# Scaling and transposing finished row pairs at other steps of the first down projection

## The chip, the core and the metric

The kernel runs on one core of a Trainium2 chip. The engines that matter here, with the names of the profile: PE (TensorE, matrix products; PEld is its loading of the stationary operand), DVE (VectorE), ACT (ScalarE), POOL (GpSimd) and SP (SyncE, which here only issues transfers). ACT issues transfers too; a transfer that stands in an engine's queue appears as ACTq or SPq. Every engine works through its own queue in order. If the instruction at the head of a queue waits for another engine or for a transfer, everything behind it on that engine waits too.

The metric is the time of one execution in device microseconds (us); less is better. Of several executions the median is given. The output must agree with the reference, in fp32.

## The reference

A trunk of two layers works on 256 context tokens and 1024 latent tokens, each a row of 1024 numbers. Each layer has a mixing part (attention beside a state-space scan, with a common input projection) and a feed-forward part. The change sits between the feed-forward part of the first layer and the input projection of the second. Cut to this stretch:

```python
def rmsnorm(x, w):
    xf = x.astype(jnp.float32)
    y = xf * lax.rsqrt(jnp.mean(xf * xf, axis=-1, keepdims=True) + EPS)
    return (y * w.astype(jnp.float32)).astype(x.dtype)

# end of layer 0; the same for the context rows with their own g2, w and gains
x = x + g2 * rmsnorm((silu(f @ w_gate) * (f @ w_up)) @ w_down, norm_ffn_post)
# start of layer 1
h = rmsnorm(x, norm_mix_pre) * (1 + sc1) + sh1
... h @ w_in ...
```

So a finished row of the down projection (`@ w_down`, 2816 inputs, 1024 outputs) is normalised, gated and added to its old value. The new row is normalised again, scaled and shifted, and multiplied by the next weights.

## The kernel before, in words

**Products.** Every fp32 number is kept as a high and a low part, and a product is three matrix products in a row (`mm3`): high by high at line L224, high by low at L225, low by high at L226. Weights come as fp32 through SP (L125, 512 KB for a step of the down projection). ACT makes the high part (L114), POOL the low part (L115). There are five buffers for split weights (`w_t`) and two for raw ones (`raw_t`).

**The down projection** (`down_all`). The ten blocks of 128 rows, called tiles here, are worked through in three groups: tiles 0 to 3, then 4 to 6, then 7 to 9. Tiles 0 and 1 are the context rows. These are groups 0, 1 and 2 below. In a group the inner loop runs over 22 steps `ff`, each with 128 of the 2816 inputs. A tile has two PSUM banks of 128x512, so a step of a group with three tiles has 3 x 2 x 3 = 18 matrix products. The `hid` operand of a step is loaded by SP at L1197 into `hid_ring`, eight steps ahead. PSUM has two pools, one of five banks (`ps_w`) and one of three (`ps_s`). A group of three tiles takes four of the one and two of the other, so one bank of each is left over.

**The end of a group.** At step 21 each tile goes through `finish_psum` and `postnorm`. ACT squares its two banks (L239), POOL forms the reciprocal root of the mean (`rstd_t`, L241, L231, L232), DVE multiplies the banks by it and by the gate row into an `xt` buffer (L828, the two instructions that free the banks). SP loads the old row (L825). The two are added at L834, by POOL for even tiles and by DVE for odd ones, and ACT's queue stores the sum at L835. There are six `xt` buffers.

**The pairs.** When the second tile of a pair (0 and 1, 2 and 3, 4 and 5, 6 and 7, 8 and 9) is finished, `done` prepares the pair for layer 1. `pre_scale` squares the new rows (ACT, L239, two for each tile), forms `rstd_t` on POOL and scales the rows in place there (L371). Because it writes in place, L371 also waits until the store L835 of the same buffer has landed. `flip_steps` then transposes the pair in four steps. A step has four transposes on PE (L398) into one `ps_w` bank, two scale-and-shift instructions on ACT (L401), the high part on POOL (L405) and the low part on DVE (L406):

```python
    def pre_scale(self, xs):
        for a in xs:
            r = self.row_rstd(...)                  # ACT L239 x2, POOL L241, L231, L232
            for b in ...:
                self.nc.gpsimd.tensor_scalar(b, b, r, 1.0, op0=ALU.mult, op1=ALU.mult)   # L371
```

In the program `down_all` calls `fill` after each step of groups 1 and 2, and `fill` takes one of the waiting flip steps. Whatever is left after group 2 is handed on as `late`. The input projection of layer 1 (`xbc(1)`) runs it inside the first column blocks, before the matrix products that need the last span of rows (`hb`, tiles 6 to 9). Its products are copied out of PSUM by ACT (L479).

**What sets the order.** The program's text is only a start. A scheduler simulates the engines and writes each engine's queue, so a change of the text moves instructions on all five queues. The rows of these queues are shown below.

Of the kernel before, what the change touches and what calls it, by code (L numbers as in the profile page):

```python
# [54 lines left out]
class Trunk:  # L55
# [1146 lines left out]
    def down_all(self, l, hx, load, fill=lambda: None, done=lambda t, x: None):  # L1202
        loads = self.loads
        ahead = 9 if l else 8
        for n in range(3, ahead):
            load(n)
        for n, (g, ff) in enumerate(loads):
            ts = self.GROUPS[l][g]
            if ff == 0:
                banks = [[a(), b()] for a, b in ((self.psw, self.psw), (self.psw, self.psw), (self.pss, self.pss), (self.psw, self.pss))[:len(ts)]]  # L1210
            h, u = hx.pop(n), self.U[l, "d", g, ff]
            for i, t in enumerate(ts):
                for c in range(2):
                    s = slice(c * 512, (c + 1) * 512)
                    self.mm3(banks[i][c], (h[:, 0, i * P:(i + 1) * P], h[:, 1, i * P:(i + 1) * P]), (u[:, 0, 0, s], u[:, 1, 0, s]),
                             ff == 0, ff == NFF - 1)
                if ff == NFF - 1:
                    done(t, self.finish_psum(l, t, banks[i]))
            self.free(l, "d", g, ff)
            load(n + ahead)  # L1220
            if g:
                fill()

    def finish_psum(self, l, t, halves):
# [7 lines left out]
def emit(nc, tc, I, out, dump=None):  # L1232
    with ExitStack() as es:
        k = Trunk(nc, tc, es, I, out)
        k.hT, k.fgrow = {}, (None, None)
        k.plan()
        SC, SA, SB = k.SPANS
        tiles = list(range(NT))
        step = lambda g: lambda *a: next(g, None)
        k.silu_c()  # L1240
        flips = [k.pre_pair(SC, 0, -1, 0, 0), k.pre_pair(SA, 0, -1, 0, 0)]
        k.mod_first()
        k.pump()
        flips[0]()
        flips[1]()
        k.pre_pair(SA, 1, -1, 0, 0)()
        late = [lambda i=i: k.pre_pair(SB, i, -1, 0, 0)() for i in range(2)]
        def drain(*gs):
            for g in gs:
                for _ in g:  # L1250
                    pass

        for l in range(DEPTH):
            ms = k.mod_stream(0, (2, 3, 4), k.psw) if l == 0 else iter(())
            k.load_qkw(l)
            k.xbc(l, step(ms), late)
            with tc.tile_pool(name=f"kv{l}", bufs=1, reuse_waits="tile") as kv:
                k.dt_raw = k.cst.tile([P, NT, 8], F32, tag="dt_raw", name="dt_raw")
                qt = tiles if l == 0 else tiles[NCT:]
                tab = k.rope_tab(k.x(), "k_norm", l)  # L1260
                k.w_tok(l, "kv", 264, tiles, lambda t, p: k.kv_proc(l, t, p, tab), step(ms))
                k.ssd_prep(l, kv)
                tabq = k.rope_tab(k.grp.tile([P, D], F32, tag="grow", name="rope_q"), "q_norm", l)
                st = k.ssd_states(l, kv)
                k.w_tok(l, "q", 512, qt, lambda t, p: k.q_proc(l, t, p, tabq), lambda: (next(ms, None), next(st, None)))
                drain(ms, st)
                cols = k.mod_cols(l, 1)
                fl = {}

                def early(stage):  # L1270
                    keep = k.hf_d[l]
                    if stage == 0:
                        cols()
                        fl[0] = k.pre_pair(SC if l == 0 else SA, 0, 2 * l, l, 1, keep if l else None)
                        if l:
                            fl[2] = [k.row_halves(t, 2) for t in (6, 7)]
                    elif stage == 1:
                        fl[0]()
                        fl[1] = k.pre_pair(SA, l, 2 * l, l, 1, keep)
                        if l:  # L1280
                            k.pre_scale(fl[2])
                    else:
                        fl[1]()
                        if l == 0:
                            fl[2] = k.pre_pair(SA, 1, 0, 0, 1, keep)

                gate, ss = k.ssd(l, kv)
                zf = itertools.chain([step(ss)] * (len(qt) - 1), [lambda: None])
                nz = iter(range(len(qt)))
                att = []  # L1290

                def zfill():
                    i = next(nz)
                    if i == 2:
                        k.att_keys(l)
                    if i == len(qt) - 4:
                        k.att_open(l)
                    if i == len(qt) - 2:
                        att.append(k.attention(l, early))
                        next(att[0])  # L1300
                    next(zf)()

                k.qs = {}
                k.w_tok(l, "z", 512, qt, gate, zfill)
                att = att[0]
                next(att)
                for _ in ss:
                    next(att)
            with tc.tile_pool(name=f"att{l}", bufs=1, reuse_waits="tile") as atp:
                try:  # L1310
                    att.send(atp)
                except StopIteration:
                    pass
            if dump and dump(k, l):
                return
            with tc.tile_pool(name=f"acc{l}", bufs=1, reuse_waits="tile") as accp:
                if l == 0:
                    B = {}

                    def fill_c():  # L1320
                        fl[2]()
                        yield
                        xs = [k.row_halves(t, 0) for t in (6, 7)]
                        B.update(k.blocks(accp))
                        yield
                        for i in range(2):
                            k.pre_scale(xs)
                            yield
                            for _ in k.quads(0, xs, i, B):
                                yield  # L1330
                            if i == 0:
                                xs = [k.row_halves(t, 0) for t in (8, 9)]
                                yield

                    fc = fill_c()
                    k.ctx_gateup(0, fc)
                    drain(fc)
                    k.back22(B)

                    def fill_s():  # L1340
                        yield from k.mod_stream(0, (5,), k.psw, True)
                        yield from k.mod_stream(1, (0, 1), k.psw, True)
                        cols = k.mod_cols(1, 0)
                        yield from k.mod_stream(1, (2,), k.psw, True)
                        cols()
                        yield from k.mod_stream(1, (3, 4, 5), k.psw, True)

                    fs = fill_s()
                    hx, load = k.ffn(0, B, step(fs), accp)
                    drain(fs)  # L1350
                    k.frow = [k.gate_row(0, 5, "norm_ffn_post", 0), k.gate_row(0, 5, "norm_ffn_post", 1, k.x())]
                    ys, todo = {}, []
                    pairs = {1: (SC, 0), 3: (SA, 0), 5: (SA, 1), 7: (SB, 0), 9: (SB, 1)}

                    def done(t, y):
                        ys[t] = y
                        if t in pairs:
                            xs = [ys[t - 1], y]
                            k.pre_scale(xs)
                            todo.append(k.flip_steps(xs, *pairs[t], 1, 0))  # L1360

                    def flip():
                        while todo and next(todo[0], todo) is todo:
                            todo.pop(0)

                    k.down_all(0, hx, load, flip, done)
                    late = [lambda: drain(todo.pop(0))] * len(todo)
                else:
                    B = k.blocks(accp)
                    B["B22"] = k.block22()  # L1370
                    k.down_all(1, *k.ffn(1, B, lambda: None, accp, fl[2], [k.last_x[t] for t in (8, 9)]))
# [23 lines left out]
```

## Time and profile before

| | us |
|---|---|
| median of 3 runs | 3227.97 |
| lowest and highest of them | 3227.72, 3238.06 |
| the profiled execution's own time | 3234.53 |
| its span in the trace | 3232.7 |
| PE busy in it | 3041.5 (94%) |
| the down projection's group 1 (from 1626.4 to 1725.3) | 98.9 |
| the down projection's group 2 (from 1725.3 to 1832.5) | 107.2 |

The trace is one execution, and its times are counted from the start of its span. Its own time is 6.56 us above the median. What is outside the span is 3234.53 - 3232.7 = 1.83 us. A row of a timeline gives the start, the duration, the engine, the line, the operation, its output and input, how many like it follow one another, and in brackets how long the engine had stood idle before and what ended that. A row of windows gives the stretch, its length, the busy time with the number of instructions, the granted PE clock (1.00 is full), the share of the transfer engines that was busy, and GB/s. `L371` is line 371 of the kernel before.

### The profile page before, as it was taken

Reading aid. Unit: us, or ns where it says so; the run is one execution under the profiler, and the core shown is the slowest. Engines: PE = TensorE matmul, PEld = TensorE weight load, DVE = VectorE, ACT = ScalarE, POOL = GpSimd, SP = SyncE. Lnnn points to the kernel's source line nnn. Section 1 sums busy time; section 2 is a strip of 40 time slices with the busy share of each in tenths; the row PEclk is TensorE's granted clock in tenths of the full one; section 3 lists DMA queues with packets and bytes.
Section 4 is the critical chain, followed back from the end, with each engine's and each line's share of the span. In section 5 each row is a group of like instructions: output and inputs, shape, how many; then the busy total and the mean of one; then the engine's idle time right before and its main releaser. Section 6 shows DMA issues by size and latency. Waiting matters only on the chain.

```text
span 3232.7 us, 44982 instructions
## 1 busy us (share of the span) xinstructions
PE 3041.5 (94%) x16147; PEld 2517.7 (78%) x16147; DVE 1665.7 (52%) x3093; ACT 1410.9 (44%) x2595; POOL 1663.6 (51%) x1529
## 2 busy tenths in 40 slices
PE   6899899999888999999998998899999899999997
PEld 4677688888787777778876778788888688888885
DVE  2557556777553655553021156759665766554003
ACT  4433337667653333332143344337666633333232
POOL 4327465555654444444476643755444555554653
PEclk8899899999999999999999999999999899999999
DMA  6267553222565554446566515653222443336766
GB/s 229 71 216 229 188 171 105 84 66 72 170 207 179 169 189 156 171 170 235 181 227 230 169 51 166 216 172 113 66 66 79 137 131 117 111 110 209 237 241 213
DMA packets 372703, 510.66 MB, mean 158 GB/s; under 512 B 25400, under 2 KB 258520, under 8 KB 372224
## 3 DMA queue, kind: packets, MB, share of 16 engines
q1 hardware_dynamic: 292912, 385.09, 37.9%
q10 hardware_dynamic: 79568, 122.69, 10.3%
q8 instruction: 128, 2.10, 0.3%
q14 instruction: 95, 0.78, 0.1%
HBM read 384.71 MB, written 122.99 MB: 157 GB/s over the span
## 4 chain that ended last, share of the span: by engine, by line
PE 73%; DMA 9%; DVE 6%; POOL 5%; ACT 3%; issue 3%; SPq 0%; ACTq 0%; DVEq 0%; POOLq 0%
PE ps_w L224 11%; PE ps_w L225 11%; PE ps_w L226 11%; PE ps_s L224 7%; PE ps_s L225 7%; PE ps_s L226 7%; PE ps_w L912 5%; PE ps_w L905 4%; PE ps_s L883 4%; POOL w_t L115 3%; DMA raw_t<-in_w_down 2%; DMA raw_t<-in_w_up 2%; ACT w_t L114 1%; PE ps_w L275 1%; PE ps_w L755 1%
## 5 line engine op out<-in xcount | busy, mean ns | idle before, releaser
L115 POOL TENSOR_TENSOR w_t<-raw_t,w_t 128x512 fp32r<-128x512 f32 (+2 forms) x430 | 795.7, 1861 | 834.3 <-ACT w_t L114 806.1
L114 ACT CAST w_t<-raw_t 128x512 fp32r<-128x512 f32 (+2 forms) x490 | 389.3, 810 | 774.4 <-PE ps_s L226 240.5
L884 DVE TENSOR_SCALAR_CACHE_REDUCE att_a<-ps_s 128x512 f32<-128x512 f32 (+1 forms) x400 | 227.0, 586 | 138.4 <-PE ps_s L883 128.1
L892 POOL TENSOR_SCALAR att_a<-att_a,att_st 128x1280 f32<-128x1280 f32 (+1 forms) x144 | 181.7, 1264 | 152.3 <-DVE att_st L891 84.2
L225 PE MATMUL ps_w<-w_t,hid_ring 128*128 128x512 f32 x523 | 207.5, 397 | 8.6 <-POOL w_t L115 8.6
L226 PE MATMUL ps_w<-w_t,hid_ring 128*128 128x512 f32 x523 | 206.3, 395 | 0.0
L224 PE MATMUL ps_w<-w_t,hid_ring 128*128 128x512 f32 x523 | 195.9, 395 | 3.7 <-ACT w_t L114 3.1
L905 PE MATMUL ps_w<-cst_all,att_a 128*128 128x128 f32 x1312 | 198.4, 277 | 0.0
L890 ACT ACTIVATE att_a<-att_a,att_st 128x1280 f32<-128x1280 f32 (+1 forms) x144 | 183.2, 1273 | 32.9 <-DVE att_st L889 30.6
L485 DVE SCALAR_TENSOR_TENSOR xt<-row,convw,xt 128x512 f32<-128x512 f32 (+1 forms) x128 | 125.1, 1031 | 84.5 <-ACT xt L483 66.0
L905 PEld LDWEIGHTS ps_w<-cst_all,att_a 128*128 128x128 f32 x1312 | 153.9, 142 | 10.7 <-DVE xt L828 5.4
L828 DVE SCALAR_TENSOR_TENSOR xt<-ps_w,rstd_t,gate_row 128x512 f32<-128x512 f32 x57 | 40.0, 746 | 230.8 <-POOL rstd_t L232 168.8
L115 DVE TENSOR_TENSOR w_t<-raw_t,w_t 128x1024 fp32r<-128x1024 f32 (+1 forms) x60 | 69.9, 1173 | 168.9 <-ACT w_t L114 168.9
L115 DVE TENSOR_TENSOR xt<-s2t,xt 128x512 fp32r<-128x512 f32 (+2 forms) x144 | 121.7, 846 | 48.2 <-ACT xt L114 46.6
L114 ACT CAST xt<-s2t 128x512 fp32r<-128x512 f32 (+2 forms) x144 | 78.0, 542 | 147.3 <-DVE s2t L1141 61.9
L224 PE MATMUL ps_w<-ha,w_t 128*128 128x512 f32 x352 | 138.5, 394 | 2.3 <-ACT xt L1016 2.3
L225 PE MATMUL ps_w<-ha,w_t 128*128 128x512 f32 x352 | 138.8, 394 | 2.0 <-DVE ha L406 2.0
L226 PE MATMUL ps_w<-ha,w_t 128*128 128x512 f32 x352 | 138.2, 393 | 0.0
L225 PEld LDWEIGHTS ps_w<-w_t,hid_ring 128*128 128x128 f32 x523 | 98.9, 189 | 34.0 <-POOL w_t L115 12.0
L224 PE MATMUL ps_w<-hc,w_t 128*128 128x256 f32 x352 | 106.1, 302 | 19.6 <-ACT w_t L114 17.6
L224 PEld LDWEIGHTS ps_w<-w_t,hid_ring 128*128 128x128 f32 x523 | 98.7, 189 | 26.8 <-ACT w_t L114 4.0
L226 PEld LDWEIGHTS ps_w<-w_t,hid_ring 128*128 128x128 f32 x523 | 98.9, 189 | 21.4
(364 smaller groups left out, 8771.3 us busy)
## 6 DMA issues: line engine op xcount, KB each, us to landing
raw_t<-in_w_down SPq DMA_DIRECT2D x132, 512.0 KB
hid<-xt ACTq DMA_DIRECT2D x88, 512.0 KB
raw_t<-in_w_gate SPq DMA_DIRECT2D x70, 512.0 KB
raw_t<-in_w_up SPq DMA_DIRECT2D x66, 512.0 KB
hid_ring<-hid SPq DMA_DIRECT2D x85, 384.0 KB
xt<-in_w_mod SPq DMA_DIRECT2D x56, 512.0 KB
xt<-xs SPq DMA_DIRECT2D x36, 512.0 KB
raw_t<-in_w_in SPq DMA_DIRECT2D x32, 512.0 KB
```

The source lines that it names most:

```text
L114: self.nc.scalar.copy(hi, src)
L115: (eng or self.nc.vector).tensor_tensor(lo, src, hi.bitcast(F32), op=ALU.subtract)
L224: mm(out, st[0], mv[0], start=first, stop=False)
L225: mm(out, st[0], mv[1], start=False, stop=False)
L226: mm(out, st[1], mv[0], start=False, stop=last)
L485: nc.vector.scalar_tensor_tensor(acc, row[:, o0 + k:o0 + k + n], cw[:, ct, k:k + 1], acc, op0=ALU.mult, op1=ALU.add)
L883: nc.tensor.matmul(s[:, :m], qs[t][c][:, hd], kst[:, g, j:j + m], start=c == 0, stop=c == 1)
L884: nc.vector.tensor_scalar(pb[:, j:j + m], s[:, :m], -0.125, None, op0=ALU.mult, op1=ALU.min, accum_out=st[:, n:n + 1])
L890: nc.scalar.activation(pb, pb, AF.Exp, bias=nmx, scale=-1.0, accum_out=st[:, 4:5])
L892: nc.gpsimd.tensor_scalar(pb, pb, st[:, 5:6], 1.0, op0=ALU.mult, op1=ALU.mult)
L905: nc.tensor.transpose(tp[:, (2 * k + h) * P:(2 * k + h + 1) * P], pr[h][:, (k2 + k) * P:(k2 + k + 1) * P], self.ident)
L912: nc.tensor.matmul(av, vst[:, kt, g], pt[:, c, k * 256:(k + 1) * 256], start=kt == 0 and c == 0, stop=kt == nk - 1 and c == 1)
```

## The change

A small generator, `ready`, stands for a pair in the list of waiting work. Its first call runs `pre_scale`, its second does nothing, and calls three to six are the four flip steps. `fill` is no longer called after step 0 of a group.

```diff
@@ down_all @@
             self.free(l, "d", g, ff)
             load(n + ahead)
-            if g:
+            if g and ff:
                 fill()
@@ emit @@
+                    def ready(xs, span, i):
+                        k.pre_scale(xs)
+                        yield
+                        yield
+                        yield from k.flip_steps(xs, span, i, 1, 0)
+
                     def done(t, y):
                         ys[t] = y
                         if t in pairs:
-                            xs = [ys[t - 1], y]
-                            k.pre_scale(xs)
-                            todo.append(k.flip_steps(xs, *pairs[t], 1, 0))
+                            todo.append(ready([ys[t - 1], y], *pairs[t]))
```

In the program's text this gives, for each pair:

| pair | scaled before | first flip before | scaled now | flips now |
|---|---|---|---|---|
| 0, 1 | end of group 0 | group 1, step 0 | group 1, step 1 | group 1, steps 3 to 6 |
| 2, 3 | end of group 0 | group 1, step 4 | group 1, step 7 | group 1, steps 9 to 12 |
| 4, 5 | end of group 1, before tile 6 is finished | group 1, step 21 | end of group 1, after tile 6 is finished | group 2, steps 2 to 5 |
| 6, 7 | group 2, step 21, before tile 8 | group 2, step 21 | group 2, step 21, after tile 9 | in `late` |
| 8, 9 | group 2, step 21 | in `late` | in `late` | in `late` |

The number of instructions on PE is the same. In the rows below a name ends in its buffer's number.

**PE, from group 1 into group 2, before.** `ps_s_15183` is a bank of tile 9, `ps_w_15179` the first of tile 7, `xt_15101` the row block of tile 4, `w_t_15011` the weight of step 0 and `w_t_15165` that of step 4.

```order
L226 MATMUL ps_s_15183<-w_t_15059,hid_ring_13732 128x512
L224 MATMUL ps_s_15183<-w_t_15083,hid_ring_13733 128x512
L225 MATMUL ps_s_15183<-w_t_15083,hid_ring_13733 128x512
L226 MATMUL ps_s_15183<-w_t_15083,hid_ring_13733 128x512
L224 MATMUL ps_s_15183<-w_t_15165,hid_ring_13732 128x512
L225 MATMUL ps_s_15183<-w_t_15165,hid_ring_13732 128x512
L226 MATMUL ps_s_15183<-w_t_15165,hid_ring_13732 128x512
L398 MATMUL ps_w_15169<-cst_all_84,xt_15101 128x128
L224 MATMUL ps_w_15179<-w_t_15011,hid_ring_13732 128x512
```

**The same place now.** The queue of group 2 begins with steps 0 to 3 on two banks. The first transpose of the pair stands behind 81 matrix products of the group:

```order
L224 MATMUL ps_w_15171<-w_t_15149,hid_ring_13732 128x512
L225 MATMUL ps_w_15171<-w_t_15149,hid_ring_13732 128x512
L398 MATMUL ps_w_15247<-cst_all_84,xt_15101 128x128
L226 MATMUL ps_w_15171<-w_t_15149,hid_ring_13732 128x512
L224 MATMUL ps_w_15172<-w_t_15149,hid_ring_13732 128x512
L225 MATMUL ps_w_15172<-w_t_15149,hid_ring_13732 128x512
L226 MATMUL ps_w_15172<-w_t_15149,hid_ring_13732 128x512
L398 MATMUL ps_w_15247<-cst_all_84,xt_15121 128x128
```

Before, the transpose of tile 4 stands in front of the group's first matrix product on a `ps_w` bank, after 15 products on one `ps_s` bank. Now it stands well inside step 4 (`w_t_15149`).

**ACT at the same boundary, before.** `xt_15101` and `xt_15121` are the rows of tiles 4 and 5, `ps_s_14499` and `ps_s_14500` the banks of tile 6.

```order
L114 CAST w_t_15165<-raw_t_15163 128x1024
L835 DMA xs1_96<-xt_15101 128x1024
L835 DMA xs1_96<-xt_15121 128x1024
L239 ACTIVATE junk_90,ss_t_15127<-xt_15101 128x512 x2
L239 ACTIVATE junk_90,ss_t_15135<-xt_15121 128x512 x2
L239 ACTIVATE junk_90,ss_t_15150<-ps_s_14499 128x512
L239 ACTIVATE junk_90,ss_t_15150<-ps_s_14500 128x512
```

**And now** (the banks of tile 6 are `ps_s_14467` and `ps_s_14468`):

```order
L239 ACTIVATE junk_90,ss_t_15134<-ps_s_14467 128x512
L114 CAST w_t_15149<-raw_t_15147 128x1024
L239 ACTIVATE junk_90,ss_t_15134<-ps_s_14468 128x512
L835 DMA xs1_96<-xt_15121 128x1024
L835 DMA xs1_96<-xt_15101 128x1024
L239 ACTIVATE junk_90,ss_t_15153<-xt_15101 128x512 x2
L239 ACTIVATE junk_90,ss_t_15161<-xt_15121 128x512 x2
```

The squares of tile 6 have moved ahead of those of the pair, and the store of tile 5 ahead of that of tile 4.

**PE in the first column blocks of layer 1, before.** `ha` and `hc` are spans of the transposed rows, `w_t_15640` and `w_t_15663` the weights of the first and second block, `xt_15157` and `xt_15726` the rows of tiles 6 and 7.

```order
L226 MATMUL ps_s_15881<-ha_14662,w_t_15640 128x512
L398 MATMUL ps_w_15810<-cst_all_84,xt_15157 128x128
L398 MATMUL ps_w_15810<-cst_all_84,xt_15726 128x128
L398 MATMUL ps_w_15810<-cst_all_84,xt_15157 128x128
L398 MATMUL ps_w_15810<-cst_all_84,xt_15726 128x128
L224 MATMUL ps_s_15907<-hc_14525,w_t_15663 128x256
```

**And now:**

```order
L224 MATMUL ps_s_15854<-ha_14782,w_t_15640 128x512
L225 MATMUL ps_s_15854<-ha_14782,w_t_15640 128x512
L226 MATMUL ps_s_15854<-ha_14782,w_t_15640 128x512
L224 MATMUL ps_s_15880<-hc_14581,w_t_15663 128x256
L225 MATMUL ps_s_15880<-hc_14581,w_t_15663 128x256
```

The four transposes have left this place. All 32 transposes of the pairs 6, 7 and 8, 9 now stand in a row behind the eight column blocks of `hc` and `ha`, where 28 stood before.

## The prediction

> **What bounds the kernel now.** I read the page's shares of busy time first, then its chain of waits.
>
> ```profile
> PE 3041.5 (94%) x16147; PEld 2517.7 (78%) x16147; DVE 1665.7 (52%) x3093; ACT 1410.9 (44%) x2595; POOL 1663.6 (51%) x1529
> PE 73%; DMA 9%; DVE 6%; POOL 5%; ACT 3%; issue 3%; SPq 0%; ACTq 0%; DVEq 0%; POOLq 0%
> ```
>
> PE is busy 94% of the span and makes most of the chain. The change adds and removes no PE instruction, so it can win only PE's idle time and slow clock, or add to them. Next, what PE waited for in groups 1 and 2 and at their start (1500 to 1850 us of the span):
>
> ```profile
> PE ps_w L398 <- POOL xt L371: 12.0, 2, 8.3
> PE ps_s L225 <- POOL w_t L115: 1.9, 1, 1.9
> PE ps_w L224 <- ACT w_t L114: 1.6, 1, 1.6
> PE ps_w L225 <- POOL w_t L115: 0.8, 1, 0.8
> PE ps_w L224 <- DVE xt L828: 0.6, 1, 0.6
> ```
>
> Columns: total us, times, longest. Twelve us are two waits of a transpose for the in-place scaling L371, exactly the two instructions that the change pulls apart. PE's timeline places them:
>
> ```profile
> 1725.27 0.40 PE L224 MATMUL ps_s<-w_t,hid_ring 128*128 128x512 f32 x1
> 1730.37 0.56 PE L225 MATMUL ps_s<-w_t,hid_ring 128*128 128x512 f32 x1 [1.90 <-POOL w_t L115]
> 1739.64 0.47 PE L398 MATMUL ps_w<-cst_all,xt 128*128 128x128 f32 x1 [8.28 <-POOL xt L371]
> 1845.43 0.55 PE L398 MATMUL ps_w<-cst_all,xt 128*128 128x128 f32 x3 [3.68 <-POOL xt L371]
> ```
>
> From 1725.27 to 1730.37 PE had only 15 products on the one free `ps_s` bank. Then the transpose of tile 4 stood at the head of its queue, while the banks behind it were free already: the four L828 that free those of tiles 4 and 5 ended at 1730.25. The windows give the price (us, PE busy, clock, DMA share, GB/s):
>
> ```profile
> 1728.50:1739.60 11.10, 0.99 (x2) 0.60 0.85 323
> 1739.60:1744.50 4.90, 4.86 (x13) 0.52 0.01 2
> 1725.30:1832.50 107.20, 97.02 (x414) 0.94 0.60 196
> 1801.60:1831.00 29.40, 29.40 (x127) 1.00 0.47 135
> 1626.40:1725.30 98.90, 96.44 (x429) 1.00 0.71 239
> ```
>
> After the stall the clock stays at 0.52 for 4.90 us. Undisturbed, seven steps of 18 products take 29.40 us: 4.20 a step, 0.2333 a product.
>
> **Term 1, the boundary of groups 1 and 2.** Twenty-two steps make 92.4 us. The pair's 16 transposes fall in this group in both kernels. Later 28 of them take 3.33 us in a row:
>
> ```profile
> 1872.75 3.33 PE L398 MATMUL ps_w<-cst_all,xt 128*128 128x128 f32 x28
> ```
>
> That is 0.12 each, 1.9 for 16. Of 107.2 us, 107.2 - 92.4 - 1.9 = **12.9 us** are lost: 1.90 + 8.28 of idle time, and most of the rest at the slow clock, where 13 instructions took 4.86 us and should take 12 x 0.2333 + 0.12 = 2.9.
>
> Does the new order meet another wait there? PE's new queue has 26 products on two free banks, then those on the banks of tiles 4 and 5, needed from 1725.27 + 26 x 0.2333 = 1731.3 on. They were free by 1730.25, with DVE doing the same four L828 in the same order:
>
> ```profile
> 1727.52 2.73 DVE L828 SCALAR_TENSOR_TENSOR xt<-ps_w,rstd_t,gate_row 128x512 f32<-128x512 f32 x4 [35.57 <-POOL rstd_t L232]
> 1732.96 1.23 DVE L834 TENSOR_TENSOR xt<-xt 128x1024 f32<-128x1024 f32 x1 [2.72 <-DMA xt<-xs]
> 1742.84 1.41 DVE L828 SCALAR_TENSOR_TENSOR xt<-ps_s,rstd_t,gate_row 128x512 f32<-128x512 f32 x2 [8.65 <-POOL rstd_t L232]
> ```
>
> The second bank of tile 6 is needed after 55 products, at 1738.1. Its L828 stands on DVE behind L834 of tile 5, which waited for the transferred old row and ended at 1734.19; plus 1.41 gives 1735.6. That is 2.5 us in time.
>
> The first transpose stands after 81 products: 1744.2; the one of tile 5 at 1745.1. When are those rows scaled?
>
> ```profile
> 1730.28 2.34 POOL L834 TENSOR_TENSOR xt<-xt 128x1024 f32<-128x1024 f32 x1
> 1738.47 1.12 POOL L371 TENSOR_SCALAR xt<-xt,rstd_t 128x1024 f32<-128x1024 f32 x1 [1.23 <-DMA xs<-xt]
> 1732.65 1.89 ACTq L835 DMA_DIRECT2D xs<-xt  x2
> 1734.59 0.63 ACT L239 ACTIVATE junk<-xt 128x512 f32<-128x512 f32 x1 [7.62 <-DVE xt L834]
> 1737.60 0.60 ACT L239 ACTIVATE junk<-ps_s 128x512 f32<-128x512 f32 x1
> ```
>
> The first L371 waited for the store of its buffer, 1738.47 - 1732.65 = 5.8 us after the issue. ACT's queue now issues tile 5's store first, after 1734.2, and tile 4's about 1735.2; 5.8 later is 1741.0. The four squares take 1737.60 - 1734.59 = 3.0 and end at 1738.2, their `rstd_t` is there about 1739.5, and POOL's L834 of tile 6, put ahead of both L371, is done by 1735.6 + 2.34 = 1738.0. So the store sets the time: L371 at 1741.0 and 1742.1, done at 1742.1 and 1743.2. **The margins are 2.1 and 1.9 us.** So I take nothing as a new stall here, with the two ends 0 and 2 us for what can eat the margin:
>
> ```profile
> 1835.32 2.78 DVE L834 TENSOR_TENSOR xt<-xt 128x1024 f32<-128x1024 f32 x1
> 1837.00 2.09 POOL L371 TENSOR_SCALAR xt<-xt,rstd_t 128x1024 f32<-128x1024 f32 x1
> ```
>
> The same two operations that took 1.23 and 1.12 took 2.78 and 2.09 when they ran over one another. Two L371 stretched so are 1.9 us. [...]
>
> The weights: step 5's buffer comes free when step 0's last product ends, after about 58 of them, at 1738.9. Its low part then takes these two conversions:
>
> ```profile
> 1725.93 1.04 ACT L114 CAST w_t<-raw_t 128x1024 fp32r<-128x1024 f32 x1
> 1727.96 2.35 POOL L115 TENSOR_TENSOR w_t<-raw_t,w_t 128x1024 fp32r<-128x1024 f32 x1
> ```
>
> The raw buffers are filled ahead, so only the two conversions follow the release: 1738.9 + 1.04 + 2.35 = 1742.3. PE needs it at 1746.8. Steps 6 and 7 have 5 to 6 us in hand by the same count.
>
> **Term 2, group 1.** In the window of 98.9 us PE was busy for 96.44, which 396 products (92.4) and 32 transposes (3.8) explain: 2.5 are lost, 1.62 + 0.79 = 2.4 of them in pauses for late weights. SP is why:
>
> ```profile
> 1633.33 9.32 SPq L825 DMA_DIRECT2D xt<-xs  x2
> 1659.38 1.20 PE L224 MATMUL ps_w<-w_t,hid_ring 128*128 128x512 f32 x4 [1.62 <-ACT w_t L114]
> ```
>
> Two loads of old rows waited 9.32 us for buffers, with weight loads queued behind. In the new order the weights of steps 4 to 7 come, by the same working as above, 6 to 8 us before PE needs them, since two banks are worked four steps ahead. I take **-2.4**; the ends are 0 and -2.5.
>
> **Term 3, the end of group 2 and layer 1's first blocks.** The 3.68 us wait goes, because the four transposes leave that place, and with it the slow clock behind it:
>
> ```profile
> 1832.40:1835.40 3.00, 3.00 (x25) 2.83 (x23) 1.49 (x3) 1.05 (x1) 2.78 (x18) 1.00 0.77 203
> 1845.43:1850.18 4.75, 4.75 (x27) 4.75 (x28) 3.56 (x5) 1.02 (x2) 4.39 (x8) 0.64 0.00 0
> ```
>
> A block of 24 products of 256 columns takes 2.9 us at full clock (25 in 3.00), and three transposes 0.4; here the 27 took 4.75 at 0.64: 1.4 lost. Gain 5.1. Against it:
>
> ```profile
> 1835.91 0.50 PE L224 MATMUL ps_s<-ha,w_t 128*128 128x512 f32 x1 [0.46 <-ACT row L479]
> 1872.75:1879.60 6.85, 4.30 (x33) 3.45 (x31) 3.90 (x5) 6.65 (x15) 4.18 (x6) 1.00 0.00 0
> 1873.43 6.49 ACT L401 ACTIVATE s2t<-ps_w,cols 128x256 f32<-128x256 f32 x14
> ```
>
> The first copy L479 comes later on ACT, estimated behind one square more (0.60 as above, and its read-out): 0.7 beyond the 0.46. A `ps_s` bank of tile 9, freed behind the same squares, is late by an estimated 0.5. Eight flip steps instead of seven stand before the `hb` products, and ACT, 14 L401 in 6.49 us, sets their pace: 0.93 a step, taken as 1.0. The new `late` scaling of tiles 8 and 9 stands on POOL about a rope product that waits for its transfer:
>
> ```profile
> 1853.59 2.40 POOL L530 TENSOR_TENSOR rope_q<-rope_q,q_norm 128x1024 f32<-128x1024 f32 x1 [3.11 <-DMA rope_q<-in_rope]
> ```
>
> Behind it the two L371 would be done by 1856.0 + 2 x 1.12 = 1858; the transposes that need them start no earlier than 1872.75 - 5.1 = 1867.6. It is hidden with some 9 us in hand. Sum: -5.1 + 0.7 + 0.5 + 1.0 = **-2.9**.
>
> [...]
>
> **The sum.** -12.9 - 2.4 - 2.9 = -18.2, and 1 back, half of the 0 to 2 above: **-17.2**. The profiled execution's 3234.53 would become 3217.3. The median shown is 6.56 lower, 3227.97, and becomes **3211**.
>
> **Rivals.**
>
> *The stall moves to the flips in group 2.* The margins are only 2 us. If both L371 take 2.09 (+1.9), the DVE add that the stores wait for takes 2.78 (+1.6), and one more L115 of 2.35 gets in front of them on POOL, they slip by 5.9 and PE stops for 3.8 to 4 us. Behind a stop as long (3.68) the clock fell, at a loss of 1.4, and after the longer one of about 2. So some 6 us come back, -17.2 + 6 = -11: **3217**, or 3221 if the store takes 4 us longer as well. Against: in the new order only the L834 of tile 6 stands between, and it is in the count.
>
> *Weights become late.* The 11.10 us stall moved data at 323 GB/s while PE stood still. Without it group 2 has to be fed as group 1 was. If the pauses of group 1 stay (+2.4) and come in group 2 as well (+2.5), it is -17.2 + 4.9 = -12.3: **3216**. Against: step 5's weight has 4.5 us in hand.
>
> *Slower: the transfers don't keep up.* A step needs 512 KB of weights and 384 KB of `hid`, 0.917 MB in 4.20 us, 218 GB/s. Two banks are now worked ahead, so all five weight buffers are held until some 58 products are through and come free within a few us; nothing is in stock after that. It decides below 218 GB/s: at 180 a step lasts 5.1, 0.9 more, in some 17 steps of both groups +31, so -17.2 + 31 = +14: **3242**. For: group 2 as a whole moved 196. Against: that was with its last loads long done, and 239 GB/s were moved over all of group 1.
>
> *The change doesn't do what it says.* The pair 4, 5 is not scaled at the second step of group 2: `fill` runs at step 21 of group 1, so its scaling starts at the old place, only after tile 6. If PE still reaches the flips as early as before, term 1 falls away: -17.2 + 12.9 = -4.3, **3224**. Against: 81 products stand before the first transpose.
>
> **How the numbers follow.** Forecast 3211 (its own range 3204 to 3217) 0.66; flips late, 3217 to 3221, 0.13; weights late, 3216, 0.08; transfers too slow, 3242, 0.07; stall kept, 3224, 0.06. A measurement of this kernel tells a change from none at about 0.3%, 9.7 us, so faster means below 3218.3. That holds for all of the forecast, half of the late flips (0.06) and nearly all of the late weights (0.07): 0.79. Within 0.3%: 0.07 + 0.01 + 0.06 = 0.14. Slower: 0.07. Without the 1 given back and the costs in term 3 (2.2) it would be 3208; since one execution and the median differ by 6.56 here, I set the range's low end at 3203. Its high end, 3221, takes in both late cases. Some 0.2 lies outside.
>
> **What the changed profile would show.** Term 1: no wait of L398 for L371 at the start of group 2, a window of group 2 of 94 to 96 us, clock 1.00 throughout. Term 2: no PE pause for L114 or L115 in group 1, about 96 us. Term 3: no wait of L398 between the first column blocks, ACT's L401 in one run of 16, and the wait for L479 about 1.1. Wrong would be: L398 waiting for L371 over 2 us at the fifth step of group 2; L224 or L225 waiting for L114 or L115 there, above all if repeated at every step; or a stop of SP at L825 of over 9 us in either group.

## The result, and the profile after

| | before | after |
|---|---|---|
| median of 9 runs each, us | 3233.1 | 3220.57 |
| lowest and highest | 3227.72, 3244.53 | 3205.48, 3225.51 |
| ratio to before, 95% interval | | 0.995 (0.9934 to 0.9966) |
| profiled execution's own time | 3234.53 | 3211.85 |
| span | 3232.7 | 3210.0 |

The ratio is 16 us less (11 to 21), where 17.2 were forecast. A second comparison, run beside an experiment below, gave 0.9932 (0.9911 to 0.9954). The change makes the kernel faster, by more than the 0.3% that a measurement can tell.

The page of the changed kernel, PE and the chain:

```profile
PE 3030.8 (94%) x16147; PEld 2506.7 (78%) x16147; DVE 1662.1 (52%) x3093; ACT 1410.2 (44%) x2595; POOL 1657.5 (52%) x1529
PE 73%; DMA 8%; DVE 7%; POOL 4%; ACT 3%; issue 3%; SPq 0%; ACTq 0%; DVEq 0%; POOLq 0%
```

The shares look as before; only a stage by stage comparison shows the change. What PE waited for from 1600 us to the first `hb` products (total, times, longest):

```profile
PE ps_s L224 <- POOL hb L405: 2.1, 1, 2.1
PE ps_s L224 <- DVE xt L828: 0.7, 1, 0.7
PE ps_w L224 <- DVE xt L828: 0.6, 1, 0.6
PE ps_s L224 <- ACT row L479: 0.5, 1, 0.5
PE ps_s L225 <- DVE hb L406: 0.3, 1, 0.3
PE ps_w L398 <- ACT s2t L401: 0.3, 1, 0.3
```

L398 no longer waits for L371 at all, and no product of the two groups waits for L114 or L115. The stages by PE's windows (us, busy, clock, DMA share, GB/s), in order group 1, group 2, the blocks up to the first `hb` product, the first 96 `hb` products. Before:

```profile
1626.45:1725.27 98.82, 96.41 (x428) 1.00 0.71 240
1725.27:1832.40 107.13, 96.95 (x413) 0.94 0.60 196
1832.40:1878.04 45.64, 39.54 (x226) 0.96 0.28 93
1878.04:1900.62 22.58, 21.99 (x95) 1.00 0.13 32
```

After:

```profile
1626.87:1722.81 95.94, 95.94 (x429) 1.00 0.75 250
1722.81:1817.25 94.44, 94.44 (x415) 1.00 0.68 219
1817.25:1858.77 41.52, 37.98 (x226) 1.00 0.30 102
1858.77:1882.41 23.64, 23.34 (x95) 0.93 0.12 30
```

The differences are -2.88, -12.69, -4.12 and +1.06: **-18.6 us** for the stretch. In groups 1 and 2 PE is now busy from end to end at full clock, so no idle time or slow clock is left to win there. The last row is worse than before: the `hb` products run at a clock of 0.93. The remaining 4 us of the 22.7 between the two spans lie outside the stretch, and the runs of one kernel differ by more than that there (last section).

The scaling and the transposes in the changed kernel:

```profile
1737.96 2.24 POOL L371 TENSOR_SCALAR xt<-xt,rstd_t 128x1024 f32<-128x1024 f32 x2 [0.96 <-DMA xs<-xt]
1741.71 0.27 PE L398 MATMUL ps_w<-cst_all,xt 128*128 128x128 f32 x1
```

The two L371 end at 1740.20. The first is done by about 1739.1 (1.12 us each), and PE comes to its transpose at 1741.71: 2.6 us in hand.

### The profile page after: what moved, and what is told of

It reads as the page before. It is cut to its first block, busy times and chain, and to the rows that moved or that the text cites. A ratio compares the mean times of both kernels' runs of the same rounds, so it can differ in the third digit from the quotient of the medians.

```text
span 3210.0 us, 44981 instructions
## 1 busy us (share of the span) xinstructions
PE 3030.8 (94%) x16147; PEld 2506.7 (78%) x16147; DVE 1662.1 (52%) x3093; ACT 1410.2 (44%) x2595; POOL 1657.5 (52%) x1529
## 3 DMA queue, kind: packets, MB, share of 16 engines
q1 hardware_dynamic: 292912, 385.09, 38.6%
## 4 chain that ended last, share of the span: by engine, by line
PE 73%; DMA 8%; DVE 7%; POOL 4%; ACT 3%; issue 3%; SPq 0%; ACTq 0%; DVEq 0%; POOLq 0%
PE ps_w L224 12%; PE ps_w L226 11%; PE ps_w L225 11%; PE ps_s L224 7%; PE ps_s L225 7%; PE ps_s L226 7%; PE ps_w L912 5%; PE ps_w L905 4%; PE ps_s L883 4%; DMA raw_t<-in_w_up 2%; POOL w_t L115 2%; PE ps_w L275 1%; ACT w_t L114 1%; DMA raw_t<-in_w_down 1%; DVE w_t L115 1%
## 5 line engine op out<-in xcount | busy, mean ns | idle before, releaser
L115 POOL TENSOR_TENSOR w_t<-raw_t,w_t 128x512 fp32r<-128x512 f32 (+2 forms) x430 | 786.5, 1840 | 824.5 <-ACT w_t L114 793.8
L114 ACT CAST w_t<-raw_t 128x512 fp32r<-128x512 f32 (+2 forms) x490 | 389.3, 810 | 779.1 <-PE ps_s L226 243.7
L115 DVE TENSOR_TENSOR w_t<-raw_t,w_t 128x1024 fp32r<-128x1024 f32 (+1 forms) x60 | 70.8, 1188 | 169.7 <-ACT w_t L114 169.6
L115 DVE TENSOR_TENSOR xt<-s2t,xt 128x512 fp32r<-128x512 f32 (+2 forms) x144 | 123.9, 861 | 49.2 <-ACT xt L114 46.3
L114 ACT CAST xt<-s2t 128x512 fp32r<-128x512 f32 (+2 forms) x144 | 78.0, 542 | 143.4 <-DVE s2t L1141 60.7
L225 PEld LDWEIGHTS ps_w<-w_t,hid_ring 128*128 128x128 f32 x523 | 98.3, 188 | 33.0 <-POOL w_t L115 11.0
L828 DVE SCALAR_TENSOR_TENSOR xt<-ps_w,rstd_t,gate_row 128x512 f32<-128x512 f32 x57 | 39.9, 746 | 159.4 <-POOL rstd_t L232 158.6
L883 PE MATMUL ps_s<-att_c,raw_q 128*128 128x512 f32 (+1 forms) x400 | 110.0, 374 | 7.5 <-DMA raw_q<-q 7.1
L224 PEld LDWEIGHTS ps_w<-w_t,hid_ring 128*128 128x128 f32 x523 | 98.0, 188 | 23.6 <-ACT w_t L114 1.2
```

What stands on the lines that cost most here:

```text
L114: self.nc.scalar.copy(hi, src)
L115: (eng or self.nc.vector).tensor_tensor(lo, src, hi.bitcast(F32), op=ALU.subtract)
L224: mm(out, st[0], mv[0], start=first, stop=False)
L225: mm(out, st[0], mv[1], start=False, stop=False)
L883: nc.tensor.matmul(s[:, :m], qs[t][c][:, hd], kst[:, g, j:j + m], start=c == 0, stop=c == 1)
```

## The experiments

Each is read by the same stages. "End" is the stage from the first `hc` product to the first `hb` product. All values are us in the trace. Seven of these kernels were timed once only, and single times of one program differ by up to 25 us (last section), so the stages are compared and not the totals.

| kernel | group 1 | group 2 | end | 96 `hb` products |
|---|---|---|---|---|
| before | 98.8 | 107.1 | 45.6 | 22.6 |
| changed | 95.9 | 94.4 | 41.5 | 23.6 |
| before, no flip step at step 21 of group 1 | 98.5 | 99.2 | 50.2 | 24.1 |
| before, flip step on another bank | 97.2 | 104.1 | 51.2 | 22.4 |
| changed, pair 4, 5 as before | 95.9 | 107.2 | 41.5 | 24.6 |
| changed, flip step at step 21 again | 95.9 | 103.2 | 41.5 | 23.7 |
| changed, one empty step less, calls from step 0 | 95.9 | 94.4 | 41.5 | 24.0 |
| changed, pairs 0 to 3 as before | 98.6 | 94.4 | 41.5 | 24.2 |
| changed, pair 6, 7 as before | 95.8 | 94.2 | 46.7 | 22.6 |
| changed, longer scaling | 95.9 | 94.4 | 42.4 | 24.0 |
| changed, last flips spread | 95.9 | 94.4 | 38.6 | 21.6 |

A few matmul records are missing from some traces, so that a boundary can be off by some tenths.

**Pair 4, 5 put back.** In the changed kernel:

```diff
-                            todo.append(ready([ys[t - 1], y], *pairs[t]))
+                            xs = [ys[t - 1], y]
+                            if t == 5:
+                                k.pre_scale(xs)
+                                todo.append(k.flip_steps(xs, *pairs[t], 1, 0))
+                            else:
+                                todo.append(ready(xs, *pairs[t]))
```

> The changed kernel with pair 4, 5 alone handled as before: scaled as soon as tile 5 is finished, first flip step at step 21 of group 1. Theory: the wait of L398 for L371 at the start of group 2 is back at 8 to 10 us with the slow clock behind it; group 1 95.9, group 2 107, the end 41.7; 12.9 more than the changed kernel. Rival (group 2 gained by other weights or other steps): group 2 at 100 or less.

Group 2 of this kernel, its waits and its window:

```profile
PE ps_w L398 <- POOL xt L371: 9.4, 1, 9.4
PE ps_s L225 <- POOL w_t L115: 1.0, 1, 1.0
1724.86:1832.04 107.18, 96.73 (x415) 0.95 0.60 193
```

As the theory said, within 0.2 us (107.2 for 107): the whole gain of group 2 comes from this pair.

**One call left out of the kernel before.** This asks whether the place of the flip alone does it:

```diff
-            if g:
+            if g and (g, ff) != (1, NFF - 1):
                 fill()
```

> The kernel before, with one call left out: no flip step at step 21 of group 1. Scaling stays at once, the two other places stay as before. Its PE queue has the first transpose of tile 4 behind 67 products of group 2 and that of tile 5 behind 75. Theory (the stall came from the transposes' place in PE's queue and from the PSUM bank that the early step took): scaled rows at 1739.6 and 1742.3 as before, wanted at 1725.3 + 67 x 0.2333 = 1740.9 and 1742.8, so no wait of L398 for L371; group 1 98.8 us, group 2 94.3 to 96, the end (start of layer 1 to the first hb product) 45.6; 11 to 13 us less than before in all. Rival (the scaling itself has to move, as in the change): L398 waits over 3 us, group 2 is 99 or more.

The time is 0.9981 of before (0.9963 to 1.0), and group 2 takes 99.2 us. Neither expectation fits: the long wait is gone, as the theory had it, but 4.8 us are lost against the changed kernel, 3.7 of them in small waits. The waits of its group 2, and its group 2 and end as windows:

```profile
PE ps_w L398 <- POOL xt L371: 1.5, 2, 1.0
PE ps_w L225 <- POOL w_t L115: 1.0, 2, 0.8
PE ps_s L224 <- DVE xt L828: 0.8, 1, 0.8
PE ps_w L224 <- ACT w_t L114: 0.4, 1, 0.4
1709.87:1809.08 99.21, 95.60 (x414) 1.00 0.63 206
1809.08:1859.26 50.18, 40.24 (x227) 0.93 0.29 95
```

Here the pair is scaled ahead of tile 6's normalisation, as in the kernel before, and that makes the things queued behind it late:

```profile
1729.84 1.41 DVE L828 SCALAR_TENSOR_TENSOR xt<-ps_s,rstd_t,gate_row 128x512 f32<-128x512 f32 x2 [9.74 <-POOL rstd_t L232]
1731.33 2.40 POOL L834 TENSOR_TENSOR xt<-xt 128x1024 f32<-128x1024 f32 x1 [1.52 <-DVE xt L828]
1734.13 2.00 ACT L114 CAST w_t<-raw_t 128x1024 fp32r<-128x1024 f32 x2 [3.18 <-POOL xt L834]
```

The two L828 that free tile 6's banks begin 20.0 us after the start of group 2 at 1709.87. In the changed kernel they begin 8.2 us after it (1731.04 - 1722.81). POOL's addition follows, and the two weight casts stand on ACT behind the store of that sum. So tile 6's second bank and the weights for two steps are late.

And then the end took 50.2 us, 4.5 more than before, with a wait of L398 for L371 of 6.12. A likely reason stands in SP's queue, where the old rows of tiles 7 to 9 are loaded behind six weights of layer 1:

```profile
1793.24 19.52 SPq L125 DMA_DIRECT2D raw_t<-in_w_in  x6
1812.82 0.57 SPq L825 DMA_DIRECT2D xt<-xs  x1
```

The load of the old row goes out 3.7 us after the first `hc` product (1812.82 - 1809.08). In the kernel before it was 0.03 us after it, in the same place of the queue. PE had gained 8 us and the chain of weights, POOL's L115 and SP's loads had not, so the addition, the store and L371 came that much later for PE. That is read from the trace; no kernel took it apart further.

**Only the flip put back.** The other half of the same question: scaling after tile 6 as in the change, flip step at step 21 as before. The cut shows the lines added, but for `xs`.

```diff
+                            todo.append(k.flip_steps(xs, *pairs[t], 1, 0) if t == 5 else ready(xs, *pairs[t]))
+                        if t == 6:
+                            k.pre_scale([ys[4], ys[5]])
```

> The changed kernel with one thing of before for pair 4, 5: the first flip step is called at step 21 of group 1, while the scaling stays after tile 6 as in the change. 30 products on the two banks of tile 9 now stand ahead of the first transpose. Theory (place of the flip and place of the scaling each cost, and the first flip step's ps_w bank is what takes the products away): PE has 15 products, then waits for tile 6's second bank, free some 9.5 us after the group's start, then 15 more, then waits for L371, done some 16.3 us after it: 6 and 3.3 us idle and some slow clock, group 2 104 to 107, the end 41.5. Rival (only the place of the scaling matters): group 2 at 99 or less.

Group 2 takes 103.2 us, just below the expected range. Its waits:

```profile
PE ps_s L224 <- DVE xt L828: 4.0, 1, 4.0
PE ps_w L398 <- POOL xt L371: 1.8, 1, 1.8
PE ps_s L225 <- POOL w_t L115: 1.0, 1, 1.0
```

PE idles 4.0 us for tile 6's second bank (6 expected) and 1.8 us for L371 (3.3 expected), the two waits that the theory named. With the two kernels above, group 2 reads:

| group 2, us | flip step at step 21 | flips later |
|---|---|---|
| pair scaled ahead of tile 6 | 107.1 | 99.2 |
| pair scaled after tile 6 | 103.2 | 94.4 |

So both halves are needed. (The upper right kernel also treats the other pairs as before; the two places put back further down leave group 2 at 94.2 and 94.4, so that does not matter here.) Later flips are worth 7.9 or 8.8 us, the later scaling 3.9 or 4.8, and they nearly add up.

**Another bank for the early flip step.** In the kernel before, the flip step at step 21 takes the fifth `ps_w` bank. Here it takes a `ps_s` bank:

```diff
-            t = ps()
+            t = self.pss() if span[0] == "ha" and i == 1 and l == 1 and k2 == 0 else ps()
```

> The kernel before, with one PSUM bank changed: the first flip step of pair 4, 5, still called at step 21 of group 1, takes a ps_s bank in place of the fifth ps_w bank. Group 2 then starts on a ps_w bank, and 60 products stand ahead of the first transposes. Theory (the bank that the early step takes is what leaves PE with 15 products): transposes wanted at 1725.3 + 60 x 0.2333 = 1739.3, tile 4 scaled 1739.6, tile 5 1742.3: a wait of about 3 us and some slow clock; group 2 97 to 100, group 1 98.8, the end 45.6. Rival (the step at 21 is too early on whatever bank): a stall of 8 us or more, group 2 105 or more.

Group 2 took 104.1, between the two expectations. The wait for L371 was 3.9 in two pieces, as the theory had it (3); waits for L115, L114 and L828 of 2.8 and a clock of 0.98 were not expected. So with the pair scaled ahead of tile 6 the bank is worth 3.0 us of group 2 (107.1 to 104.1), and leaving the early step out 7.9: the bank that it takes is part of its price and not all. The end was late here too (51.2).

**The empty step.** In the changed kernel:

```diff
                         k.pre_scale(xs)
                         yield
-                        yield
                         yield from k.flip_steps(xs, span, i, 1, 0)
@@
-            if g and ff:
+            if g:
                 fill()
```

> The changed kernel without the empty step and with calls from step 0 on: the pair is scaled at step 21 as in the changed kernel, and flipped at steps 0 to 3 of group 2, two steps earlier. Theory (the scheduler places the transposes by when it reckons the rows scaled, and the empty steps do nothing): 81 products stand ahead of the first transpose again; group 1 95.9, group 2 94.3, the end 41.7, within 1 us of the changed kernel. Rival (the empty steps give the scaling its time): two steps are 8.4 us, of which 2.6 were in hand, so a stall of 5.8 and 2 of slow clock, group 2 at 102.

```profile
1721.60:1816.04 94.44, 94.44 (x415) 1.00 0.68 219
```

The same 94.44. The empty step and the call that is left out after step 0 do nothing for PE: its first transpose stands behind 81 products either way. What counts is that scaling comes after tile 6 and that no flip step is called before group 2.

**Group 1 put back.** Pairs 0, 1 and 2, 3 as in the kernel before, inside the changed one. The lines left out are as in the first diff of this section:

```diff
+                            if t < 4:
+                                k.pre_scale(xs)
+                                todo.append(k.flip_steps(xs, *pairs[t], 1, 0))
@@
-            if g and ff:
+            if g == 1 or g and ff:
                 fill()
```

> The changed kernel with pairs 0, 1 and 2, 3 handled as before: scaled at the end of group 0, flipped from step 0 of group 1 on. Theory (their scaling ahead of the last tile's additions keeps row buffers longer, SP waits 9 us for them and the weights behind come late): SP's wait at L825 is back at 9 us, pauses of PE for L114 and L115 of 2.4 us in all, group 1 98.8 in place of 95.9; group 2 94.3, the end 41.7. Rival (the pauses differ from run to run): group 1 near 96.

The waits of PE in its group 1, and SP's stop:

```profile
PE ps_w L224 <- ACT w_t L114: 1.4, 1, 1.4
PE ps_w L225 <- POOL w_t L115: 0.8, 1, 0.8
1634.28 9.33 SPq L825 DMA_DIRECT2D xt<-xs  x2
```

As the theory said: SP's stop of 9.3 us and the pauses of 2.2 us are back. In the changed kernel SP issues the same two loads singly and waits 3.3 us at most for POOL's L834.

**The end put back.** Pair 6, 7 as in the kernel before, `t == 7` in place of `t == 5` in the first diff of this section.

> The changed kernel with pair 6, 7 alone handled as before: scaled once tile 7 is finished, first flip step at step 21 of group 2. Theory: its four transposes stand between the first column blocks again and wait 3 to 4 us for L371, with the slow clock behind; the end 45.6 in place of 41.7, group 1 95.9, group 2 94.3. Rival (the end gained because everything before it came earlier): the end stays under 43.

```profile
PE ps_w L398 <- POOL xt L371: 3.8, 1, 3.8
```

The wait is back, and the end takes 46.7 us. That the rest came earlier did not shorten it.

**A longer scaling.** Tiles 4 and 5 are multiplied by 1.0 twice more on POOL. The cut shows the loop alone; `again` is 2 for this pair and 0 for the others.

```diff
+                for _ in range(again):
+                    self.nc.gpsimd.tensor_scalar(b, b, 1.0, 1.0, op0=ALU.mult, op1=ALU.mult)
```

> The changed kernel with the rows of tiles 4 and 5 multiplied by 1.0 twice more on POOL after L371, four instructions of 1.12 us, 4.5 in all. The scheduler moves the first transpose behind 121 products for it. Theory (POOL has slack there once the transposes may stand later): group 2 within 1 us of 94.3. Rival (the margins of 2 us decide: the low parts of the weights for steps 5 to 7, queued behind on POOL, come late): PE waits for L115 2 to 4 us, group 2 96.5 to 99.

Group 2 took 94.4 again, with the four instructions at 1.05 each behind L371 and between the L115 of the weights. The scheduler had moved the first transpose behind 121 products (28.2 us after the group's start), so this shows slack on POOL and not how small the margin of the transposes may be. The end was 0.9 longer (42.4), through the waits for L479 and L828 (0.98 and 1.13 in place of 0.49 and 0.72); why is open.

**Spreading the last flips.** The changed kernel lets all 32 transposes of the last two pairs stand in a row. Here two flip steps stand behind each of the last four column blocks:

```diff
+            for at, (span, ct) in enumerate(first if l == 0 else sorted(first, key=lambda a: a[1])):
                 mm(ct, rows[ct], span)
+                for _ in range((0, 0, 1, 1, 2, 2, 2, 0)[at] if l else 0):
+                    next(late_steps, None)
```

The cut shows the calls alone. `late_steps` first scales pair 8, 9, then goes through an empty step and the eight flip steps in order; the last two are run behind the eighth block by `late`.

> The changed kernel with the eight flip steps of pairs 6, 7 and 8, 9 spread: two each behind the last four of the eight column blocks of hc and ha (the scaling of 8, 9 earlier in the program), where the changed kernel has all 32 transposes in a row behind the blocks. Theory (ACT's 16 scale-and-shift instructions in a row, 7.4 us, set the pace there, while ACT is nearly idle during the blocks): the waits of 0.26, 2.08 and 0.30 us before the hb products fall to under 1 in all; the end 41.7 to 39.3 us, groups 1 and 2 as in the changed kernel; some 2.4 less than it. Rival (the flips delay ACT's copies of the blocks and so the ps_s banks): new waits for L479 of 1 to 2 us, no gain.

Its end and its first `hb` products, two windows of PE, and one of the four places where ACT now does its scale-and-shift work:

```profile
1818.32:1856.90 38.58, 37.41 (x225) 1.00 0.32 110
1856.90:1878.60 21.70, 21.70 (x99) 1.00 0.15 37
1850.41 1.93 ACT L401 ACTIVATE s2t<-ps_w,cols 128x256 f32<-128x256 f32 x4
```

The end is 2.9 us shorter than in the changed kernel, and the 96 `hb` products 2.0 us shorter: 0.3 is the wait for L406 that is gone, and most of the rest is the clock, 1.00 in place of 0.93. Time: 0.9908 of before (0.9886 to 0.993). Both kernels were then run side by side:

> The changed kernel once more, beside the kernel with spread flips, on one chip. Expected 0.995 of before, from its first comparison (0.9934 to 0.9966).

> The kernel with spread flips once more, beside the changed kernel on one chip. Theory: by its windows it is 2.9 us shorter than the changed kernel in the end stage and alike elsewhere, so 0.999 of it, 0.994 of before. Rival: its first comparison, 0.9908 of before (0.9886 to 0.993), means a gain of 13 us more than the changed kernel somewhere outside the stretch.

The changed kernel gave 0.9932 (0.9911 to 0.9954), the spread one 0.9916 (0.9891 to 0.9941). The windows were those of the first time: 94.44, 38.60 and 21.63. So it is some 5 us shorter in the stretch (2.9 and 2.0), and both comparisons put it ahead of the changed kernel, but side by side the intervals overlap: by total time alone it could not be told from it. The expectation had left out the 2.0 us in the `hb` products; the 13 us of its rival were scatter.

## Why the prediction was right

**Term 1, -12.9; measured -12.69.** The loss was where the prediction put it, and nothing took its place. The allowance of 1 us for a new wait was not needed: the two L371 did not run into DVE (2.24 for both), and the first was late only by its store, as argued. The margin was 2.6 us against 2.1. What the prediction could not separate is how the term is made up: 7.9 to 8.8 for the flips and 3.9 to 4.8 for the scaling behind tile 6. Its reasoning spoke of the transposes alone, and that half alone (the kernel with one call left out) brought 7.9 us in group 2, most of which the stages behind lost again: 0.9981 of before in all.

**The weights' margin was wrong.** The step said that only the two conversions follow the release of a buffer, with 4.5 us in hand for step 5. In the trace of the changed kernel:

```profile
1740.15 4.75 POOL L115 TENSOR_TENSOR w_t<-raw_t,w_t 128x1024 fp32r<-128x1024 f32 x2
1744.94 0.39 PE L225 MATMUL ps_w<-w_t,hid_ring 128*128 128x512 f32 x1
1746.96 1.05 ACT L114 CAST w_t<-raw_t 128x1024 fp32r<-128x1024 f32 x1 [2.67 <-DMA raw_t<-in_w_down]
```

The low part of step 5 began on POOL only behind both L371, and was done at about 1742.5 against PE's need at 1744.94: 2.4 us in hand. The cast of step 7 waited for its transfer, so the raw buffers are not filled as far ahead as assumed. It was enough, but nearer to the second rival than the prediction thought.

**Term 2, -2.4; measured -2.88.** The pauses named are gone, and putting group 1 back brought SP's stop at L825 and the pauses back together. That the stop alone makes the pauses is not shown: the scaling and the first flips of these pairs moved with it, and the kernel with the flip step on another bank, which treats these pairs as the kernel before does, has one pause only, of 1.1 us, and a group 1 of 97.2.

**Term 3, -2.9; measured -4.12 up to the first `hb` product and +1.06 in the 96 behind it, -3.06 in all.** The sum is right by errors that cancel. The gain was put too low. From the first of the four transposes to the end of the wait and of the block behind it was 8.70 us (1841.48 to 1850.18); the block now takes 2.98 (1827.32 to 1830.30), so 5.7 are won and not 5.1. Another 0.3 is one product, L462, that stood inside this stage and now stands just ahead of it. Of the costs, the wait for L479 was 0.49 and not about 1.1; the bank of tile 9 cost 0.72 against 0.5; the eighth flip step about 0.85 (four transposes at 0.12, a wait of 0.26, 0.1 more behind it) against 1.0.

And one cost is not in the sum: the clock. The prediction's row for this place in the kernel before (1872.75 to 1879.60) has a clock of 1.00, and no loss was added for the new order. The traces with 32 transposes in a row took 23.6, 23.7, 24.0, 24.0, 24.2, 24.2 and 24.6 us for the 96 products, all seven above the 22.6 of before. Of the four with 28 in a row three kept 22.4 to 22.6 and one, the kernel with one call left out, took 24.1. With eight in a row and no wait, two of two took 21.6.

The windows around the last flips and the first `hb` products, in the changed kernel and then in the kernel before:

```profile
1852.45:1856.04 3.59, 3.33 (x30) 1.00 0.00 0
1856.04:1858.77 2.73, 0.65 (x5) 1.00 0.00 0
1858.77:1860.32 1.55, 1.25 (x3) 0.66 0.00 0
1860.32:1863.00 2.68, 2.68 (x7) 0.56 0.00 0
1863.00:1868.00 5.00, 5.00 (x24) 1.00 0.00 0
```

```profile
1872.75:1876.10 3.35, 3.33 (x29) 1.00 0.00 0
1876.10:1878.04 1.94, 0.00 (x0) 1.00 0.00 0
1878.04:1879.60 1.56, 0.97 (x4) 1.00 0.00 0
1879.60:1882.00 2.40, 2.40 (x10) 1.00 0.00 0
1882.00:1887.00 5.00, 5.00 (x23) 1.00 0.00 0
```

In both the transposes themselves ran at 1.00. In the changed kernel PE then waited 0.26, 2.08 and 0.30 us, and the first `hb` products ran at 0.66 and 0.56. In the kernel before it waited 1.97 and 0.59 us, and they ran at 1.00. The length of the wait alone does not decide: the kernel with one call left out has 28 transposes and waits of 1.97 and 0.58 us too, and its `hb` products had a clock of 0.93 (1859.26 to 1883.40). What does decide is not shown.

So the prediction was wrong to add nothing for the clock behind the 2 us wait. How much of the +1.06 is the change's own is open. All seven traces with its order were slow there, but so was one of the four with 28 transposes in a row, so the one profiled execution of the kernel before may have been lucky.

**The rivals.** Late flips: L398 waited for L371 nowhere. Late weights: no wait for L114 or L115. Too slow transfers: group 1 moved 250 GB/s and group 2 219 with PE at work throughout, above and at the 218 that the rival named as the limit. That the pair is not scaled at the second step of group 2 was right as to the text, and it costs nothing, as the kernel without the empty step shows.

The forecast of 3211 was made from a median of 3227.97. The later runs of the kernel before lie higher, at 3233.1, and those of the changed kernel at 3220.57; the ratio, 0.995, against 0.9947 forecast, is the better measure. Taken alone, 3220.57 lies above the forecast's own 3204 to 3217 and among the times given to late flips; it is the waits of the profile, and not the time, that rule these out.

## What to carry to other kernels

Where an instruction that waits for a long chain stands in an in-order queue ahead of work that is ready, price the queue and not the instruction: here one transpose of 0.3 us cost 8 us. Look at what the early step takes (a PSUM bank) and what it stands in front of on every engine, since moving the transposes alone brought 7.9 of 12.7 us, and the stages behind gave 6.1 of them back (50.2 + 24.1 against 45.6 + 22.6); by the trace, their own chain of loads was no earlier. A wait of 2 us can cost more than itself: read the clock in the products behind it (over the 96 `hb` products 0.93 in the changed kernel, behind 2.08 us, and 1.00 in the spread one, with no wait).

## What was not expected of the hardware

The total times of one program differ by up to 25 us from run to run (3192.56 to 3217.72 for the spread kernel), while the windows of the stretch repeat to 0.1 us: group 2 took 94.44 in six traces. Of the 20.2 us between the two profiled runs of the spread kernel (spans 3211.0 and 3190.8), 16.7 are there before the stretch begins (group 1 starts at 1627.95 and at 1611.21). Their first 200 us as PE's windows, the slower one first:

```profile
0.00:200.00 200.00, 159.59 (x905) 0.91 0.49 155
0.00:200.00 200.00, 169.51 (x1003) 0.94 0.54 170
```

The faster run had 98 more recorded instructions through PE by then, and moved 170 GB/s where the other moved 155. One wait of PE is nearly as long as the 9.9 us that lie between the busy times: before 1600 us the slower run's L275 waited 9.3 us at a stretch for a transfer (`raw_m`), the faster one's 0.3 at most. In the kernel before and the changed kernel that wait, 9.1 and 8.9 us, lies in the first 200 us. The spread kernel's second trace and that of the kernel with one call left out start group 1 10 us or more ahead of the others (1611.21 and 1611.36 against 1621.55 and later). No version here touches that transfer, and why it is late is open. A change of 5 us can be read from windows in a kernel whose totals can't show it.
